# A hybrid encoder layer on one core: one more fused pair, another order of pairs, and a fifth head under way

## The chip, the cores and the metric

The kernel runs on one core of one Trainium2 chip. The metric is the device time of one execution in microseconds (us), lower is better. TensorE (PE) multiplies matrices, VectorE (DVE) and ScalarE (ACT) work elementwise, GpSimd (POOL) and SyncE (SP) issue transfers here.

## The reference, cut to what matters

```
xn = rms_norm(x, norm_g)                      # x: 256 x 4096
h = xn @ w_in                                 # w_in: 4096 x 14336
c_val, c_glu, c_gate, q, k, v, a_gate = split(h)   # seven parts of 2048 columns
conv_out = conformer_conv(c_val, c_glu, ...) * silu(c_gate)   # GLU, depthwise conv31, LayerNorm, swish
q, k = rms_norm per head (16 heads of 128)
attn = longnet_mixture(q, k, v, rel_bias)     # three dilated windows, merged by their softmax denominators
mixed = concatenate([conv_out, attn * silu(a_gate)])
y = x + mixed @ w_out                         # w_out: 4096 x 4096
```

Everything is float32. The two large products with w_in and w_out are nearly all of the work; every weight is read once.

## The kernel before, in words

**Numbers in two parts.** TensorE gets each float32 number as a high part and a low part, and a product is three products: high by high, low by high (activations' low part), high by low. The activations' parts are made once; those of the weights are made as they arrive, and this is what VectorE and ScalarE do most of the time.

**Groups, pairs and slots.** The weights are cut into 18 groups of 1024 columns: groups 0 to 3 are the convolution's values with their GLU halves, 4 and 5 its gates, 6, 7, 9 and 11 queries and keys (qk0 to qk3), 8, 10, 12 and 13 attention gates with values (agv0 to agv3), 14 to 17 the output. A group has 16 pairs; a pair is two tiles of 128 rows by 1024 columns, loaded as one tile `raw` by the SP queue, three pairs ahead. The pairs of a group are taken in the order `ORDERS[g]`, so slot 13 of a group holds pair `ORDERS[g][13]`. `raw109` is slot 13 of group 6 (16 x 6 + 13).

**A plain pair** (`plain`, L1325 and L1327) takes 24 matmuls of 128 x 512. First come 16 with the high part of the weights, `wh`, then 8 with the low part, `wl`. Its split is two casts on ScalarE (`wh`, L1131) and one subtraction on VectorE (`wl`, L1137).

**A fused pair** (`fused`) multiplies the two by two blocks of a pair by Strassen's scheme in Winograd's form: 7 products of blocks in place of 8, so 21 matmuls. Three products first (L1192 to L1194), then `m5`, `m7`, `m6` and `c21` with the high parts of `t1`, `t3`, `t2`, `t4` (two matmuls each, L1296 and L1298), then the four with the low parts (one each). Its split has four steps (`split_fused`): `b`, `b22` and three sums of blocks in place of `raw` (L1163, L1175, L1176), `t13`, `t42`; each of `b`, `b22`, `t13`, `t42` is a cast on ScalarE and a subtraction on VectorE. The sums of the activations' blocks (`xs`, `ms`) are made once for each fused pair (`block_sums`). The fused pairs of a group are listed in `FUSED[g]`: in groups 3 to 8 pairs 2, 4, 6, 8, 10, 12, 13, in group 14 pairs 0 to 3, in 15 to 17 pairs 0 to 6.

**Where the parts lie.** The parts of the weights take turns in four buffers `ws` and four more of the pool `c4`. A step of a split is put into the program as soon as a buffer is free in the order of the program (`Stream.step`, `Stream.before`), and on the chip it waits for the last matmul that reads what lay there.

**The end of a group.** The fused pairs gather the products that several blocks share in four banks of PSUM of their own, `m1`, `m5`, `m6`, `m7`. After the last fused pair `add_more` puts a copy of `m1` (ScalarE, L1359) and four additions (VectorE, L1366, L1367, L1371, L1372) into the program, one step at a time during the next plain pair (`self.add()` in `plain`), or all at once ahead of the last slot:

```
                while self.add():
                    pass
                for e in range(2):
                    for s in range(2):
                        self.before()
                        self.plain_last(u, j, rows, s, e, one)
```

In the last slot `plain_last` (L1341, L1343) finishes the four quarters of the result one after the other, 6 matmuls each, the fifth and sixth of which read `wl`. Each quarter is then taken out of PSUM (`evacuate_sum`: L981 on VectorE, L984 or L987 on ScalarE; `add_out`, L943, in the output). The next group's quarters lie in the banks that held `m1`, `m6`, `m7`, `m5`.

**Work beside the stream.** Lanes of generators (`pump`) put the rest between the matmuls: the convolution's products (`cp`, L562, `cT`, L596 and L628, `a`, L507), squares for the norms (L757), and the heads. `head_lane` has up to four heads under way at a time; each loads its bias (`T`, L789), multiplies queries and keys (`psc`, L802), takes a softmax, is turned through DRAM, and multiplies with the values (`po`, L847), then by the gate (L852). In group 14 the first fused pair waits, as the program is built, for the last head and gate (`busy()`).

Of the kernel before, what the change touches and what calls it, by code (L numbers as in the profile page):

```python
# [11 lines left out]
F32 = mybir.dt.float32  # L12
F32R = mybir.dt.float32r
# [4 lines left out]
P = 128  # L18
# [24 lines left out]
SETTLED = 3000  # L43

CP_MIN = 900
C4 = 16

X_LOAD = {0: 12, 1: 16, 3: 20, 5: 24, 6: 28}
X_SQUARE = {4: 4, 5: 0, 6: 8, 7: 12, 8: 16, 9: 20, 10: 24, 11: 28}
# [17 lines left out]
FUSED_IN = range(1, 9)  # L67
SUMS = (2, 4, 6, 8, 10, 12, 13)
FUSED = [SUMS if g in FUSED_IN else () for g in range(N_IN)]
FUSED[1], FUSED[2] = (6, 8, 12), SUMS[1:]  # L70
FUSED += [range(4)] + 3 * [range(7)]
ORDERS = N_IN * [range(16)]
ORDERS += [(8, 9, 10, 11, 12, 13, 14, 0, 15, 1, 4, 2, 5, 3, 6, 7)]
ORDERS += 3 * [(8, 9, 0, 10, 1, 11, 2, 12, 3, 13, 4, 14, 5, 6, 15, 7)]

W_SLOTS, W_MORE = 4, 4
# [61 lines left out]
def layer_kernel(  # L138
# [18 lines left out]
    sb = ctx.enter_context(tc.tile_pool(name="sb", bufs=1))  # L157
    ps = ctx.enter_context(tc.tile_pool(name="ps", bufs=1, space=bass.MemoryType.PSUM))

    def t4(name):  # L160
        return sb.tile([P, 4, 256], F32, tag="c4", bufs=C4, name=name)

    def t2(name):
        return sb.tile([P, 512], F32, tag="t2", bufs=5, name=name)

    def h2(name):
        return t2(name).rearrange("p (a b) -> p a b", a=2)
# [58 lines left out]
    def settled():  # L226

        end = now[0] + SETTLED
        while now[0] < end:
            yield  # L230
# [138 lines left out]
    def block_sums(j, src_of, parts, out, name, small=False):  # L369


        a11, a21, a12, a22 = (by_block(src_of[2 * j + k])[:, s] for k in range(2) for s in range(2))
        t = t2(f"{name}_{j}")
        s1, s2, s3, s4 = (
            t[:, P * i : P * i + P].rearrange("p (a i) -> p a i", a=4) for i in range(4)
        )
        nc.vector.tensor_sub(s1, a21, a22)
        nc.vector.tensor_sub(s2, s1, a11)
        yield 580
        nc.vector.tensor_sub(s3, a11, a21)  # L380
        nc.vector.tensor_add(s4, a12, s2)
        yield 580
        if small:
            both = [sb.tile([P, 512], F32R, tag="toep", bufs=4, name=f"{name}p{j}{i}") for i in "hl"]
        else:
            both = sb.tile([P, 2, 512], F32R, tag="c4", bufs=C4, name=f"{name}p{j}")
            both = both[:, 0], both[:, 1]
        nc.scalar.copy(both[0], t)
        yield 0, 620
        nc.vector.tensor_sub(both[1], t, both[0].bitcast(F32))  # L390
        names = {f"s{i + 1}": [b[:, P * i : P * i + P] for b in both] for i in range(4)}
        names["a11"] = [m[2 * j][:, :P] for m in parts]
        names["a12"] = [m[2 * j + 1][:, :P] for m in parts]
        names["a22"] = [m[2 * j + 1][:, P:] for m in parts]
        out[j] = names
        yield 690

    def by_block(ap):

        if len(ap.shape) == 3:  # L400
            return ap.rearrange("p t (s a i) -> p (t s) a i", s=2, a=4)
        return ap.rearrange("p (s a i) -> p s a i", s=2, a=4) if len(ap.shape) == 2 else ap
# [380 lines left out]
    def head_gen(hg, hh):  # L783
        h = 4 * hg + hh
        hs = slice(DH * hh, DH * hh + DH)
        while hg not in qk_ready:
            yield
        T = sb.tile([P, 512], F32, tag="toep", bufs=4, name=f"T{h}")
        nc.sync.dma_start(  # L789
            T[:, :384],  # L790
            bass.AP(
# [9 lines left out]
        for it in range(2):  # L801
# [7 lines left out]
        window = bass.AP(  # L809
            tensor=T.tensor, offset=T.offset + S - 1, ap=[T.ap[0], [P, 2], [-1, 256]]  # L810
        )
# [22 lines left out]
        yield from settled()  # L834
        tmp = T
        nc.vector.transpose(
# [51 lines left out]
            elif j in FUSED[-1]:  # L888
                later.append(j)

    post_lane, head_lane, gate_lane, mix_lane = Lane(2, (0,)), Lane(4), Lane(1, ()), Lane(1)
    fetch_lane, ag_lane = Lane(1, (1,)), Lane(1, ())
    conv_lane, ln_lane, cp_lane = Lane(1, ()), Lane(1, (0,)), Lane(1, (1,))
    center_lane = Lane(1, (1,))
# [103 lines left out]
    def post(g, e, tile_, pair):  # L998
        kind, idx = groups[g][:2]
        if kind == "conv" and e == 1:  # L1000
            post_lane.add(glu_post(idx, tile_))
        elif kind == "gate":
            post_lane.add(gate_post(2 * idx + e, tile_))
        elif kind == "agv" and e == 0:
            ag_lane.add(ag_post(idx, tile_))
        elif kind == "agv":
            vt[idx] = pair
        elif kind == "qk" and e == 0:
            qt[idx] = tile_
        elif kind == "qk":  # L1010
            kt[idx] = tile_
            post_lane.add(qk_norm(idx))
            for hh in range(4):
                head_lane.add(head_gen(idx, hh))
# [30 lines left out]
    class Stream:  # L1045
# [24 lines left out]
        def tile(self, name, of, tag):  # L1070

            self.held[tag] += 1
            self.tags.setdefault(of, []).append(tag)
            bufs, n = (W_SLOTS, 2048) if tag == "ws" else (C4, 1024)
            return sb.tile([P, n], F32R, tag=tag, bufs=bufs, name=name)
# [378 lines left out]
def _layout(i):  # L1454


    def cols(a):
        return a.reshape(-1, P).T

# [4 lines left out]
    for g, (kind, _, *firsts) in enumerate(GROUPS):  # L1464
# [4 lines left out]
        for j in FUSED[g]:  # L1469
            jj = (j + n_pairs // 2) % n_pairs if kind == "out" else j  # L1470
            b = w[g, jj].reshape(P, 4, 512)
            w[g, jj] = b[:, (0, 2, 3, 1)].reshape(P, 2, 2, 512)
    x_cols = i["x"][0].T.reshape(KT, P, S).transpose(1, 0, 2).reshape(P, KT * S)
    vecs = [i[n][0] for n in ("conv_b", "conv_ln_g", "conv_ln_b", "q_norm_g", "k_norm_g")]
# [4 lines left out]
        "vecs": np.concatenate([cols(v) for v in vecs], axis=1),  # L1479
        "conv_w": i["conv_w"][0].T.reshape(16, P, TAPS).transpose(1, 0, 2).reshape(P, -1),  # L1480
        "bias_rows": np.concatenate(
# [32 lines left out]
```

## Time and profile before

| what | us |
|---|---|
| median of three runs | 1561.62 |
| the three runs | 1560.17, 1561.62, 1565.84 |
| the profiled execution | 1561.59 |
| its span on the core | 1559.8 |
| TensorE busy | 1554.2 |
| VectorE busy | 1350.8 |
| ScalarE busy | 1017.3 |
| GpSimd busy | 148.5 |

The span is what the trace covers; 1.8 us of the profiled execution lie around it. Busy time of an engine is the time in which it runs instructions, so TensorE has 5.6 us without a matmul in the span. The granted clock is 1.00 of 2.4 GHz from end to end.

### The profile page before, as it was taken

Reading aid. Unit: us, or ns where it says so; the run is one execution under the profiler, and the core shown is the slowest. Engines: PE = TensorE matmul, PEld = TensorE weight load, DVE = VectorE, ACT = ScalarE, POOL = GpSimd, SP = SyncE. Lnnn points to the kernel's source line nnn. Section 1 sums busy time; section 2 is a strip of 40 time slices with the busy share of each in tenths; the row PEclk is TensorE's granted clock in tenths of the full one; section 3 lists DMA queues with packets and bytes.
Section 4 is the critical chain, followed back from the end, with each engine's and each line's share of the span. In section 5 each row is a group of like instructions: output and inputs, shape, how many; then the busy total and the mean of one; then the engine's idle time right before and its main releaser. Section 6 shows DMA issues by size and latency. Waiting matters only on the chain.

```text
span 1559.8 us, 18654 instructions
## 1 busy us (share of the span) xinstructions
PE 1554.2 (100%) x6844; PEld 1285.2 (82%) x6844; DVE 1350.8 (87%) x1449; ACT 1017.3 (65%) x1564; POOL 148.5 (10%) x222
## 2 busy tenths in 40 slices
PE   9999999999999999999999999999999999999998
PEld 8888888888888888888888888888888888888887
DVE  7898799989899888999897989886676798998988
ACT  7665556767676677677778887776657654555453
POOL 0000000101010100001120012010240200000000
PEclk9999999999999999999999999999999999999999
DMA  9556567969788887789695668665886866666663
GB/s 350 199 201 231 189 218 241 274 218 267 241 258 254 243 246 256 228 247 251 226 313 188 230 229 266 213 230 203 251 270 209 252 223 230 239 217 240 234 240 119
DMA packets 80828, 367.91 MB, mean 236 GB/s; under 512 B 9152, under 2 KB 31296, under 8 KB 44128
## 3 DMA queue, kind: packets, MB, share of 16 engines
q1 hardware_dynamic: 50336, 317.86, 57.9%
q0 software_dynamic: 30112, 48.58, 14.3%
q8 instruction: 53, 0.87, 0.2%
q14 instruction: 39, 0.32, 0.1%
q10 hardware_dynamic: 288, 0.28, 0.1%
HBM read 328.57 MB, written 18.91 MB: 223 GB/s over the span
## 4 chain that ended last, share of the span: by engine, by line
PE 94%; DVE 2%; DMA 1%; issue 1%; ACT 1%; DVEq 0%; SPq 0%; ACTq 0%
PE c L1325 40%; PE c L1327 20%; PE m L1296 6%; PE c L1341 4%; PE m L1298 3%; PE c L1296 2%; PE c L1193 2%; PE c L1194 2%; PE c L1192 2%; PE c L1343 2%; PE acc L1033 2%; PE acc L1034 2%; PE acc L1036 2%; DMA raw<-in_w_dram 1%; PE c L1298 1%
## 5 line engine op out<-in xcount | busy, mean ns | idle before, releaser
L1137 DVE TENSOR_TENSOR wl<-raw,wh 128x2048 fp32r<-128x2048 f32 x196 | 448.2, 2289 | 146.9 <-ACT wh L1131 140.3
L1131 ACT CAST wh<-raw 128x1024 fp32r<-128x1024 f32 x392 | 390.7, 1047 | 194.0 <-PE c L1327 124.0
L1325 PE MATMUL c<-wh,nh 128*128 128x512 f32 x1152 | 450.2, 391 | 0.0
L1327 PE MATMUL c<-wh,nl 128*128 128x512 f32 x1152 | 448.4, 389 | 0.0
L1154 ACT CAST t<-raw 128x1024 fp32r<-128x1024 f32 x152 | 160.1, 1053 | 250.3 <-DVE raw L1163 171.1
L1325 PE MATMUL c<-wl,nh 128*128 128x512 f32 x1152 | 287.7, 392 | 0.0
L1325 PEld LDWEIGHTS c<-wh,nh 128*128 128x128 f32 x1152 | 216.3, 188 | 45.2
L1327 PEld LDWEIGHTS c<-wh,nl 128*128 128x128 f32 x1152 | 216.3, 188 | 45.1
L1325 PEld LDWEIGHTS c<-wl,nh 128*128 128x128 f32 x1152 | 216.3, 188 | 44.9
L1155 DVE TENSOR_TENSOR t<-raw,t 128x1024 fp32r<-128x1024 f32 x152 | 185.5, 1222 | 3.7 <-ACT t L1154 0.4
L562 ACT ACTIVATE cp<-a,wT 128x241 f32<-128x241 f32 (+14 forms) x312 | 131.4, 491 | 1.0 <-DVE cT L619 1.0
L1325 PE MATMUL c<-wh,mh 128*128 128x512 f32 x280 | 109.1, 390 | 0.0
L1327 PE MATMUL c<-wh,ml 128*128 128x512 f32 x280 | 108.9, 389 | 0.0
L581 POOL DMA_DIRECT2D cT<-cp x38 | 48.8, 1285 | 533.7 <-ACT cp L562 488.7
L1163 DVE TENSOR_TENSOR raw<-raw 128x1024 f32<-128x1024 f32 x76 | 93.1, 1225 | 2.6
L1155 DVE TENSOR_TENSOR b<-raw,b 128x1024 fp32r<-128x1024 f32 x76 | 92.7, 1220 | 1.6 <-ACT b L1154 1.0
L1154 ACT CAST b<-raw 128x1024 fp32r<-128x1024 f32 x76 | 79.6, 1047 | 3.5 <-PE c L1327 1.8
L1296 PE MATMUL m<-t,xsp 128*128 128x512 f32 x216 | 72.3, 389 | 0.0
L628 DVE SCALAR_TENSOR_TENSOR cT<-a,wT,cT 128x255 f32<-128x255 f32 (+8 forms) x168 | 68.9, 476 | 0.6
L1325 PE MATMUL c<-wl,mh 128*128 128x512 f32 x280 | 69.2, 389 | 0.0
L1327 PEld LDWEIGHTS c<-wh,ml 128*128 128x128 f32 x280 | 52.6, 188 | 10.9
L1325 PEld LDWEIGHTS c<-wl,mh 128*128 128x128 f32 x280 | 52.6, 188 | 10.9
(346 smaller groups left out, 2311.0 us busy)
## 6 DMA issues: line engine op xcount, KB each, us to landing
raw<-in_w_dram SPq DMA_DIRECT2D x286, 1024.0 KB, 5.0
xr<-in_x_dram SPq DMA_DIRECT2D x8, 512.0 KB, 6.5
out_dram<-xr SPq DMA_DIRECT2D x15, 256.0 KB, 7.5
xT<-in_x_cols_dram SPq DMA_DIRECT2D x7, 512.0 KB, 9.0
T<-bias_dram SPq DMA_DIRECT2D x16, 192.0 KB, 6.1
cT<-cp POOLq DMA_DIRECT2D x4, 488.0 KB, 6.7
cT<-cp POOLq DMA_DIRECT2D x4, 486.0 KB, 6.7
cT<-cp POOLq DMA_DIRECT2D x4, 484.0 KB, 6.1
```

The source lines that it names most:

```text
L562: nc.scalar.activation(cp[:, t, lo:hi], a[:, t, lo + sh : hi + sh], AF.Copy, scale=wT[:, 4 * cb + t, k : k + 1],)
L628: nc.vector.scalar_tensor_tensor(c[:, t, lo:hi], a[:, t, lo + sh : hi + sh], wT[:, 4 * cb + t, k : k + 1], c[:, t, lo:hi], op0=ALU.mult, o ...
L1131: nc.scalar.copy(h, raw_tiles[u][:, k])
L1137: nc.vector.tensor_sub(l, src, h.bitcast(F32))
L1154: nc.scalar.copy(h, src)
L1155: nc.vector.tensor_sub(l, src, h.bitcast(F32))
L1163: nc.vector.tensor_add(r[:, 0:4:3, :], r[:, 0:3:2, :], twice(r[:, 3, :]))
L1296: nc.tensor.matmul(acc, ah, b, start=begin, stop=end)
L1298: nc.tensor.matmul(acc, al, b, start=False, stop=False)
L1325: nc.tensor.matmul(acc, a[s][0], b[e], start=begin, stop=False)
L1327: nc.tensor.matmul(acc, a[s][1], b[e], start=False, stop=False)
L1341: nc.tensor.matmul(acc, a[s][0], b[e], start=False, stop=end)
```

## The change

Five things, all in tables and pool sizes:

- In groups 3 to 8 (`FUSED_IN[2:]`) pairs 13 and 14 change places: slot 13 holds the plain pair 14, and slot 14 the fused pair 13. Before, the fused pairs 12 and 13 stood in slots 12 and 13 and the plain pairs in 14 and 15.
- In group 14 pair 4 is fused too, and the order is new: the fused pairs stand in slots 6, 8, 10, 12, 14 in place of 7, 9, 11, 13.
- Up to five heads are under way in place of four.
- `T` and the small sums (`toep`) get five buffers in place of four, and the tiles of 128 x 512 (`t2`) six in place of five.
- The pool `c4` has 15 buffers in place of 16.

```diff
-C4 = 16
+C4 = 15
...
-FUSED += [range(4)] + 3 * [range(7)]
+FUSED += [range(5)] + 3 * [range(7)]
 ORDERS = N_IN * [range(16)]
-ORDERS += [(8, 9, 10, 11, 12, 13, 14, 0, 15, 1, 4, 2, 5, 3, 6, 7)]
+for _g in FUSED_IN[2:]:
+    ORDERS[_g] = (*range(13), 14, 13, 15)
+ORDERS += [(8, 9, 10, 11, 12, 13, 0, 14, 1, 15, 2, 5, 3, 6, 4, 7)]
...
-        return sb.tile([P, 512], F32, tag="t2", bufs=5, name=name)
+        return sb.tile([P, 512], F32, tag="t2", bufs=6, name=name)
...
-            both = [sb.tile([P, 512], F32R, tag="toep", bufs=4, name=f"{name}p{j}{i}") for i in "hl"]
+            both = [sb.tile([P, 512], F32R, tag="toep", bufs=5, name=f"{name}p{j}{i}") for i in "hl"]
...
-        T = sb.tile([P, 512], F32, tag="toep", bufs=4, name=f"T{h}")
+        T = sb.tile([P, 512], F32, tag="toep", bufs=5, name=f"T{h}")
...
-    post_lane, head_lane, gate_lane, mix_lane = Lane(2, (0,)), Lane(4), Lane(1, ()), Lane(1)
+    post_lane, head_lane, gate_lane, mix_lane = Lane(2, (0,)), Lane(5), Lane(1, ()), Lane(1)
```

The changed file has two lines more ahead of the functions, so that L1359 of before is L1361 of the changed kernel.

ScalarE before, at the end of group 6: the last fused pair is `109` (slot 13), `110` and `111` are plain, `112` is the first pair of group 7, and the copy of `m1` is the first step of `add_more`.

```order
L1154 CAST t42_1090_4456<-raw109_4332 128x1024
L1131 CAST wh110_4475<-raw110_4368 128x1024 x2
L1131 CAST wh111_4490<-raw111_4411 128x1024 x2
L1359 COPY qk0_0_4521<-m1_6_4047 128x512
L1131 CAST wh112_4537<-raw112_4460 128x1024 x2
L757 ACTIVATE sq0_0_0_4581,ssqk0_4580<-qk0_0_4521 128x128
```

The same place on ScalarE in the changed kernel, where `110` is the last fused pair:

```order
L1156 CAST t42_110_4479<-raw110_4368 128x1024
L1133 CAST wh111_4501<-raw111_4411 128x1024 x2
L1133 CAST wh112_4535<-raw112_4443 128x1024 x2
L1361 COPY qk0_0_4541<-m1_6_4046 128x512
L759 ACTIVATE sq0_0_0_4581,ssqk0_4580<-qk0_0_4541 128x128
L759 ACTIVATE sq0_0_1_4583,ssqk0_4580<-qk0_0_4541 128x128
```

The copy of `m1` stood ahead of the next group's first cast (`wh112`) and now stands behind it. It is so in groups 3 to 8 and, for the copy of group 14, ahead of group 15.

VectorE before, at the same end of group 6, from the last step of the fused pair `109` on:

```order
L1155 TENSOR_TENSOR t13_109_4447<-raw109_4332,t13_109_4447 128x1024
L1155 TENSOR_TENSOR t42_1091_4457<-raw109_4332,t42_1090_4456 128x1024
L1137 TENSOR_TENSOR wl110_4480<-raw110_4368,wh110_4475 128x2048
L1137 TENSOR_TENSOR wl111_4506<-raw111_4411,wh111_4490 128x2048
L1366 TENSOR_TENSOR us6_4520<-qk0_0_4521,m6_6_4049 128x512
L1367 TENSOR_TENSOR qk0_0_4521<-us6_4520,m7_6_4050 128x512
L1371 TENSOR_TENSOR qk0_1_4522<-m5_6_4048,us6_4520 128x512
L1372 TENSOR_TENSOR qk0_1_4522<-m5_6_4048,qk0_0_4521 128x512
L1137 TENSOR_TENSOR wl112_4548<-raw112_4460,wh112_4537 128x2048
L981 TENSOR_TENSOR qk0_0_4521<-qk0_0_4521,c11_6_3960 128x512
```

VectorE in the changed kernel:

```order
L1157 TENSOR_TENSOR t13_110_4474<-raw110_4368,t13_110_4474 128x1024
L1157 TENSOR_TENSOR t42_110_4479<-raw110_4368,t42_110_4479 128x1024
L1139 TENSOR_TENSOR wl111_4512<-raw111_4411,wh111_4501 128x2048
L1368 TENSOR_TENSOR us6_4540<-qk0_0_4541,m6_6_4048 128x512
L1369 TENSOR_TENSOR qk0_0_4541<-us6_4540,m7_6_4049 128x512
L1373 TENSOR_TENSOR qk0_1_4542<-m5_6_4047,us6_4540 128x512
L1374 TENSOR_TENSOR qk0_1_4542<-m5_6_4047,qk0_0_4541 128x512
L1139 TENSOR_TENSOR wl112_4548<-raw112_4443,wh112_4535 128x2048
L983 TENSOR_TENSOR qk0_0_4541<-qk0_0_4541,c11_6_3958 128x512
```

One `wl` fewer stands between the last fused pair's split and the last slot's `wl111`, and between it and the additions that need the fused pair's banks; the additions still stand ahead of the next group's first `wl112`.

TensorE before, in group 14 ahead of its first fused pair (slot 7, `m1_14`), from the low part of slot 6 on; `po15` is the last head, and `po12` to `po14` stand some 65 rows further ahead:

```order
L1325 MATMUL c12_14_9568<-wl230_9829,mh14_9562 128x512
L1325 MATMUL c22_14_9569<-wl230_9829,mh14_9562 128x512
L1325 MATMUL c12_14_9568<-wl230_9829,mh14_9562 128x512
L1325 MATMUL c22_14_9569<-wl230_9829,mh14_9562 128x512
L847 MATMUL po15_9905<-pr15_9377,agv3_1_9551 128x256 x2
L1192 MATMUL m1_14_9917<-b_2310_9833,mh0_8948 128x512
```

TensorE in the changed kernel, in group 14 ahead of its first fused pair, now slot 6:

```order
L849 MATMUL po13_9841<-pr13_9231,agv3_1_9579 128x256 x2
L849 MATMUL po14_9844<-pr14_9244,agv3_1_9579 128x256 x2
L849 MATMUL po15_9847<-pr15_9293,agv3_1_9579 128x256 x2
L1327 MATMUL c11_14_9595<-wl229_9776,mh13_9508 128x512
L1327 MATMUL c21_14_9596<-wl229_9776,mh13_9508 128x512
L1327 MATMUL c11_14_9595<-wl229_9776,mh13_9508 128x512
L1327 MATMUL c21_14_9596<-wl229_9776,mh13_9508 128x512
L1327 MATMUL c12_14_9597<-wl229_9776,mh13_9508 128x512
L1327 MATMUL c22_14_9598<-wl229_9776,mh13_9508 128x512
L1327 MATMUL c12_14_9597<-wl229_9776,mh13_9508 128x512
L1327 MATMUL c22_14_9598<-wl229_9776,mh13_9508 128x512
L1194 MATMUL m1_14_9881<-b_2300_9780,mh0_8960 128x512
```

All four last heads stand together now, 8 matmuls ahead of the first fused pair, which begins one plain pair earlier.

## Rows read from the trace of the kernel before

**Rows 1.** The page: busy time, share of the span, instructions of each engine.

```profile
PE 1554.2 (100%) x6844; PEld 1285.2 (82%) x6844; DVE 1350.8 (87%) x1449; ACT 1017.3 (65%) x1564; POOL 148.5 (10%) x222
```

**Rows 2.** What TensorE waited for in the whole span.

```profile
PE spin L1399 <- DVE ones L174: 1.1, 1, 1.1
PE m L1296 <- ACT t L1154: 0.5, 1, 0.5
```

**Rows 3.** Timeline of TensorE, group 6, slots 11 to 13: start, duration, instruction.

```profile
571.46 1.98 PE L1325 MATMUL c<-wl,nh 128*128 128x512 f32 x8
573.27 0.39 PE L1192 MATMUL m<-b,nh 128*128 128x512 f32 x1
...
580.93 0.40 PE L1298 MATMUL m<-t,xsp13l 128*128 128x512 f32 x1
581.80 0.50 PE L1296 MATMUL m<-t,xsp13h 128*128 128x512 f32 x1 [0.48 <-ACT t L1154]
```

**Rows 4.** Timeline of VectorE, group 6, slots 11 to 13.

```profile
567.05 2.29 DVE L1137 TENSOR_TENSOR wl<-raw,wh 128x2048 fp32r<-128x2048 f32 x1 [2.64 <-ACT wh L1131]
...
573.10 0.69 DVE L1176 TENSOR_TENSOR raw<-raw 128x512 f32<-128x512 f32 x1
...
579.98 0.69 DVE L1176 TENSOR_TENSOR raw<-raw 128x512 f32<-128x512 f32 x1
```

**Rows 5.** Timeline of ScalarE, group 6, slots 10 to 13.

```profile
563.05 2.08 ACT L596 ACTIVATE cT<-a,vec_cols,wT 128x256 f32<-128x256 f32 x4
...
580.70 1.05 ACT L1154 CAST t<-raw 128x1024 fp32r<-128x1024 f32 x1 [0.95 <-DVE raw L1176]
```

**Rows 6.** Timeline of TensorE, groups 4 and 5: last slot, low parts of slots 1 and 11.

```profile
423.41 0.39 PE L1341 MATMUL c<-wh,nh 128*128 128x512 f32 x1
...
437.92 0.84 PE L1325 MATMUL c<-wl,nh 128*128 128x512 f32 x3
...
488.92 1.07 PE L1325 MATMUL c<-wl,nh 128*128 128x512 f32 x4
```

**Rows 7.** Timeline of VectorE from group 4 to group 5, and slot 11 of group 5.

```profile
419.94 0.68 DVE L1366 TENSOR_TENSOR us<-gate,m 128x512 f32<-128x512 f32 x1
...
421.86 0.68 DVE L1372 TENSOR_TENSOR gate<-m,gate 128x512 f32<-128x512 f32 x1
423.83 2.29 DVE L1137 TENSOR_TENSOR wl<-raw,wh 128x2048 fp32r<-128x2048 f32 x1 [1.29 <-ACT wh L1131]
426.04 1.28 DVE L981 TENSOR_TENSOR gate<-gate,c 128x512 f32<-128x512 f32 x2
...
432.33 2.29 DVE L1137 TENSOR_TENSOR wl<-raw,wh 128x2048 fp32r<-128x2048 f32 x1 [1.37 <-ACT wh L1131]
...
481.90 2.29 DVE L1137 TENSOR_TENSOR wl<-raw,wh 128x2048 fp32r<-128x2048 f32 x1 [0.68 <-ACT wh L1131]
```

**Rows 8.** Timeline of ScalarE from group 4 to group 5.

```profile
418.55 0.57 ACT L1359 COPY gate<-m 128x512 f32<-128x512 f32 x1
...
429.77 0.63 ACT L984 ACTIVATE gate<-gate 128x512 f32<-128x512 f32 x1 [0.73 <-DVE gate L981]
430.31 1.98 ACT L1131 CAST wh<-raw 128x1024 fp32r<-128x1024 f32 x2
```

**Rows 9.** Timeline of VectorE, slot 1 of groups 4 and 7.

```profile
348.13 2.29 DVE L1137 TENSOR_TENSOR wl<-raw,wh 128x2048 fp32r<-128x2048 f32 x1
...
597.16 2.29 DVE L1137 TENSOR_TENSOR wl<-raw,wh 128x2048 fp32r<-128x2048 f32 x1 [1.58 <-ACT wh L1131]
```

**Rows 10.** Timeline of TensorE, low part of slot 1 of groups 4 and 7.

```profile
355.38 0.84 PE L1325 MATMUL c<-wl,nh 128*128 128x512 f32 x3
...
603.75 0.62 PE L1325 MATMUL c<-wl,nh 128*128 128x512 f32 x2
```

**Rows 11.** Timeline of VectorE, group 14: the first fused pair's last step.

```profile
1260.33 2.35 DVE L1155 TENSOR_TENSOR t<-raw,t 128x1024 fp32r<-128x1024 f32 x2
```

**Rows 12.** Timeline of TensorE, group 14: start of the first fused pair.

```profile
1262.37 0.58 PE L1192 MATMUL m<-b,mh 128*128 128x512 f32 x1
```

## The prediction

> **What bounds the kernel now.** I read the page first: TensorE is busy for 1554.2 of 1559.8 us [rows 1], so only its own work, or a wait that it does not have yet, can change the time. Then its waits: 1.1 us at the start and one of 0.5 us [rows 2]. All the rest is matmuls at an even pace: eight of them, 571.46 to 573.27, make 0.2266 us each [rows 3], so a plain pair of 24 takes 5.44 us and a fused one of 21 takes 4.76. VectorE is busy for 87% [rows 1], and what it and ScalarE do for a pair has to be ready ahead of TensorE. The reader should therefore look in the timelines for one thing: how far ahead. I call **lead** the time from the end of a plain pair's `wl` on VectorE to the first matmul that reads it. In slot 11 of group 5 it is 488.92 - (481.90 + 2.29) = 4.73 us [rows 6, 7], in slot 11 of group 6 it is 571.46 - 569.34 = 2.12 us [rows 3, 4].
>
> **What lead is needed.** Behind `wl` VectorE does `b` and the sums of `raw`, which end at 573.79 [rows 4], 4.45 after the `wl`; then ScalarE casts `t42`, 1.05 us [rows 5]. TensorE reads that cast 21 matmuls, 4.76 us, after the first low matmul of the slot ahead (8 low ones, then 13 of the fused pair). 4.45 + 1.05 + some 0.1 for two handovers - 4.76 gives 0.85 us: with less lead than this in a slot that a fused pair follows, TensorE waits for the difference. The one stall shows that this counting works. Between neighbouring fused pairs VectorE needs 579.98 - 573.10 = 6.88 us [rows 4] where TensorE takes 4.76, so 2.12 is lost; 2.12 - 0.85 - 2.12 = -0.85 is forecast for slot 13 of group 6, and the row shows 581.80 - 580.93 - 0.23 = 0.64 lost [rows 3]. Two slots of plain and fused take TensorE 10.20 us; the chain from one `wl` to the next takes 4.45 + 1.05 + 1.98 (the two casts `wh`) + 2.29 + 0.1, 9.87. So a lead lost comes back by some 0.35 us every two slots; group 5 goes from 3.30 in slot 1 to 4.73 in slot 11 that way, with one step without gain.
>
> **What the change gives.** A fifth fused pair in group 14 takes out 3 matmuls: 3 x 0.2266 = 0.68 us. No two fused pairs are neighbours in group 6: 0.64. The other groups' neighbours cost nothing now, since [rows 2] has one such wait. For the 0.68 I take the row. The Trainium skill, "TensorE: Matmul & The Clock Gate", section "Back-to-back issue gap", gives about 131 ns for a matmul of 512 columns in a sustained stream; the three would give 0.39 by it, and the time would be 0.3 us longer. The trace disagrees at 227 ns, and I stay with it.
>
> **What it moves at the ends of groups.** Let T be the start of the last slot's matmuls, 423.41 in group 4 [rows 6]. Now the copy of `m1` is at T - 4.9 [rows 8], the additions from T - 3.5 to T - 0.9, the next group's first `wl` ends at T + 2.7, and the `wl` of its slot 1 at 434.62, T + 11.2; it is needed at 437.92, T + 14.5 [rows 6, 7]: lead 3.30. In the changed order the copy stands behind two casts of the next group. Their buffer is that of `t13` of the last fused pair, which the third last matmul ahead of T reads, so they start at T - 0.2. Two casts 1.98, copy 0.57 [rows 8]: T + 2.35. Additions, 421.86 + 0.68 - 419.94 = 2.60 [rows 7]: T + 4.95. `wl`, 2.2 to its successor's start: T + 7.15. Four evacuations, two of which take 1.28 [rows 7]: T + 9.6. Then ScalarE's pass over the last quarter 0.63, the casts of slot 1 1.98 [rows 8], and the `wl` 2.29: about T + 14.45. The lead is 0.05, so TensorE loses 0.85 - 0.05 = **0.8 us at 4 to 5, and the same at 5 to 6**, which has the same operations. No PSUM bank is late: the first bank given back by the additions is needed at T + 5.9, the last at T + 7.7, and they end at T + 4.95.
>
> Elsewhere the same shift, some 3.3 to 3.8 us, meets more lead. Slot 1 of group 4 has 355.38 - 350.42 = 4.96 [rows 9, 10], and keeps 1.2. Slot 1 of group 7 has 603.75 - 599.45 = 4.30 [rows 9, 10] and keeps some 0.5, and more if group 6 ends late (below). Group 8 is like 4, within 0.1 us of the limit; group 9 has no fused pairs, and VectorE needs 2.29 there for 5.44 of TensorE. From 14 to 15 the eight operations of `add_more` end near T + 6, the first `wl` at T + 8.2 against T + 9.07. For all of these I take **0.1 us**.
>
> **What it moves inside.** The last slot now follows a fused pair, and its quarters read `wl` after 4 matmuls, not after 16: 12 x 0.2266 = 2.72 us of lead go. With the gain of 0.35, slot 15 needs 2.37 in slot 13. Group 3 is entered as before; group 4 starts from 1.2 and grows by 6 steps to over 3. Group 5 starts from 0.85 and gains 5 steps: 2.6, just enough. Group 6 starts from 0.85 too, but the convolution's `cT` stands between two links of its chain, 2.08 us [rows 5]; in slot 11 it has 2.12 where group 5 has 4.73, 2.61 less. So 0.85 + 4 x 0.35 - 2.61 = -0.36 there: TensorE loses 0.85 + 0.36 = **1.2 us** at slots 11 and 12. Slot 13 then has 1.2, slot 15 has 1.2 + 0.35 - 2.72 = -1.15: **1.15 us** more at the last slot, which group 7 finds as lead. Groups 7 and 8, with their squares and norms spread over ScalarE's gaps, keep some 2.4 or more in slot 13.
>
> **The fused pairs of group 14.** The first fused split ends at 1262.68 [rows 11], 0.3 us after `m1` starts [rows 12], and the low part of `t42` is read 19 matmuls, 4.3 us, after `m1`: 4 us in hand. One slot earlier is 5.44 us earlier, and as the lists of the section on the change show, a `wl` is gone ahead of it; the sums for pair 6 and the gating of the last heads go behind it too, some 7 us in all. I take nothing. The fifth head starts work early and saves at most the changeover between heads and stream; nothing. Its cost could be a head's load landing late; from nothing to the 0.9 us of a stall like those above, I take nothing: in the order of TensorE the closest head's turned operand is asked for 31 matmuls, 7.0 us, ahead of its use, against 33 before. One buffer of `c4` fewer against two small ones more: nothing, as the buffers handed to the weights stay at four.
>
> **Sum.** 0.8 + 0.8 + 0.1 + 1.2 + 1.15 = 4.05 lost, 0.68 + 0.64 = 1.32 gained: +2.7 us on the execution's own 1561.59 (span 1559.8 and 1.8 around it), which is the median of the runs, 1561.62, within 0.03. That gives 1564.3. Each of the four stalls rests on differences good to 0.2 us, as the -0.85 against 0.64 shows, and a stall in one place is lead in the next.
>
> **Rivals.**
> *Only the gains.* The shift is absorbed, because the needed lead is smaller than 0.85, or the copy is not held so long. For it: the formula was 0.2 too strict in group 6, and the shifts are of the size of the leads. Against it: the casts stand ahead of the copy in the list. 1561.6 - 1.3 = 1560.3. The Trainium skill, "TensorE: Matmul & The Clock Gate", section "Architectural detail: the array is 16× 32×32, not 1× 128×128", says that ScalarE and VectorE take their queues strictly in order and that only TensorE can pull weight loads ahead; by that the copy cannot pass the casts, and this rival needs the leads instead. Chance 0.25.
> *Leads don't come back.* If the chain of 9.87 us takes 10.2 once the convolution's casts `cp` stand in it, every group from 4 to 8 meets its last slot with 0.85 - 2.72: 1.9 us each, 5 x 1.9 = 9.5, with the 1.7 at the boundaries 11.2 less 1.3: 1571.5. It decides once the gain per two slots falls under 0.1 us. Against it: group 5's leads grew with these casts in it. Chance 0.06.
> *The change does not do what it says in group 14.* The fifth pair is fused in the program, but the heads or their sums come late, and TensorE waits at the first fused pair for the four last heads to be gated; each VectorE operation behind them (1.5 us for four, 2.3 with a `wl`) is paid. 1564.3 + 3 = 1567.3. Against it: the 4 us in hand. Chance 0.07.
> The forecast itself has 0.62.
>
> **The numbers.** Half a per cent, 7.8 us, is about what a measurement of this kernel can tell from no change; the three runs already differ by 5.7. Forecast, only-gains and group 14 all lie inside: same 0.92. Slower holds the second rival and a little of a group 14 that goes worse: 0.07. Faster by 7.8 us isn't to be had where TensorE has 5.6 us without work: 0.01. The range goes from the only-gains case, with 0.3 for the order of the sum's errors, to 1568.5, where the third rival and one more boundary of 0.8 end; it leaves out the second.
>
> **What would show it.** 3 matmuls fewer; no wait in the pairs 12 and 13 for a neighbour; waits of TensorE for `wh` or `t` in slots 1 and 2 of groups 5 and 6, for `wh` and `t` at slots 11 and 12 of group 6, and for `wl` (L1343) at its last slot, together near 4 us; the copy of `m1` 2 us after T in groups 3 to 8; no wait ahead of `m1` in group 14. Wrong would be: no waits at all (the first rival), waits for `wl` at every last slot (the second), or a wait at `m1` of group 14 (the third).

## The result, and the profile after

The changed kernel takes 1564.68 us, median of 20 runs (1563.36 to 1566.78), the kernel before 1560.51, median of 20 (1560.10 to 1565.84). The ratio is 1.0024, with a 95% interval of 1.0018 to 1.0031: a quarter of a per cent slower, 4.2 us by the medians. The ratios leave out one run, of e10 below, which took 2874.52 us at a granted clock of 0.77. The forecast was 1564.3. The profiled execution took 1564.29 us, with a span of 1562.5.

The page and TensorE's waits of the changed kernel, which answer to [rows 1] and [rows 2]:

```profile
PE 1555.6 (100%) x6841; PEld 1282.8 (82%) x6841; DVE 1353.3 (87%) x1457; ACT 1016.5 (65%) x1563; POOL 149.7 (10%) x223
```

```profile
PE spin L1401 <- DVE ones L176: 1.1, 1, 1.1
PE c L1343 <- DVE wl L1139: 0.6, 1, 0.6
PE c L1327 <- DVE wl L1139: 0.5, 1, 0.5
PE acc L1035 <- ACT wh L1108: 0.2, 1, 0.2
PE c L1327 <- ACT wh L1133: 0.2, 1, 0.2
```

Three matmuls fewer, and where one wait stood there are several. Most of them are too short for this view. They show when one takes, for each group, the time from its first matmul to the next group's first. That is the ruler of this study: it repeats to 0.04 us from kernel to kernel wherever nothing was changed, with two exceptions. Group 6 takes 82.67 to 83.29 with its order unchanged, and with five heads groups 10 to 13 differ from execution to execution (e9 below). Each kernel has one profiled execution, so in these places a figure is good for that execution only. In us, each against the profiled execution of before:

| group | before | changed | what it holds |
|---|---|---|---|
| 4 | 82.54 | +0.08 | |
| 5 | 82.54 | +0.91 | waits in slots 1 and 2 |
| 6 | 83.29 | +1.48 | waits in slots 1, 2, 12, 15; the neighbours' wait of before gone |
| 8 | 82.54 | +0.17 | |
| 9 | 90.51 | +0.77 | a wait in slot 1, and short ones |
| 10 to 13 | 370.71 | +0.59 | a wait for `wl` in group 11; heads moved from 12 to 11 |
| 14 | 87.86 | -0.72 | 3 matmuls fewer, no wait |
| 2, 3, 7, 15 to 17 | | +0.04 together | |

The sum is +3.3. The span grew by 2.7, since the start up to group 2 was 0.60 shorter in this execution.

**From group 4 to 5.** The timeline of ScalarE in the changed kernel, which answers to [rows 8]:

```profile
422.61 2.00 ACT L1133 CAST wh<-raw 128x1024 fp32r<-128x1024 f32 x2 [0.73 <-PE m L1298]
424.52 0.58 ACT L1361 COPY gate<-m 128x512 f32<-128x512 f32 x1
430.57 2.43 ACT L986 ACTIVATE gate<-gate 128x512 f32<-128x512 f32 x4 [5.47 <-DVE gate L983]
432.90 1.97 ACT L1133 CAST wh<-raw 128x1024 fp32r<-128x1024 f32 x2
```

The timeline of VectorE there, which answers to [rows 7]:

```profile
420.40 2.29 DVE L1139 TENSOR_TENSOR wl<-raw,wh 128x2048 fp32r<-128x2048 f32 x1 [0.67 <-ACT wh L1133]
425.12 0.69 DVE L1368 TENSOR_TENSOR us<-gate,m 128x512 f32<-128x512 f32 x1 [2.43 <-ACT gate L1361]
...
427.65 2.28 DVE L1139 TENSOR_TENSOR wl<-raw,wh 128x2048 fp32r<-128x2048 f32 x1
429.85 2.48 DVE L983 TENSOR_TENSOR gate<-gate,c 128x512 f32<-128x512 f32 x4
...
434.91 2.29 DVE L1139 TENSOR_TENSOR wl<-raw,wh 128x2048 fp32r<-128x2048 f32 x1 [1.96 <-ACT wh L1133]
```

And TensorE's, which answers to [rows 6]:

```profile
422.88 0.40 PE L1343 MATMUL c<-wh,nh 128*128 128x512 f32 x1
...
433.98 0.50 PE L1327 MATMUL c<-wh,nh 128*128 128x512 f32 x1
434.32 0.40 PE L1329 MATMUL c<-wh,nl 128*128 128x512 f32 x1
...
437.78 1.98 PE L1327 MATMUL c<-wl,nh 128*128 128x512 f32 x8
...
442.31 0.39 PE L1300 MATMUL m<-t,xsp 128*128 128x512 f32 x1
442.84 0.50 PE L1298 MATMUL m<-t,xsp 128*128 128x512 f32 x1
443.17 0.39 PE L1300 MATMUL m<-t,xsp 128*128 128x512 f32 x1
```

T, the start of the last slot's matmuls, is 422.88. VectorE is free at 422.69, waits 2.43 us for the copy behind two casts, and starts the additions at T + 2.24 (forecast 2.35). The `wl` of slot 1 ends at T + 14.32 (forecast 14.45). TensorE then loses 0.19 at the first matmul of slot 1 and 0.30 at `t42` in slot 2, and 0.11 at the matmul behind each, 0.71 in all; the rest of group 5's 0.91 is matmuls at a pace slower by up to 0.03 us each. The lead in slot 1, 437.78 - 437.20, is 0.58, and what TensorE still loses at `t42` says how much was needed: 0.88.

**The end of group 6.** VectorE and TensorE of the changed kernel:

```profile
589.56 2.29 DVE L1139 TENSOR_TENSOR wl<-raw,wh 128x2048 fp32r<-128x2048 f32 x1 [0.67 <-ACT wh L1133]
592.42 0.69 DVE L1368 TENSOR_TENSOR us<-qk,m 128x512 f32<-128x512 f32 x1 [0.57 <-ACT qk L1361]
```

```profile
590.86 0.40 PE L1345 MATMUL c<-wh,nl 128*128 128x512 f32 x1
591.90 0.73 PE L1343 MATMUL c<-wl,nh 128*128 128x512 f32 x2 [0.64 <-DVE wl L1139]
592.47 0.39 PE L1343 MATMUL c<-wh,nh 128*128 128x512 f32 x1
```

The last slot's fifth matmul waits for a `wl` that ends at 591.85: 0.81 us, and 0.11 behind it.

**In group 11**, which the forecast did not have, VectorE and TensorE of the changed kernel:

```profile
955.18 1.30 DVE L489 STREAM_TRANSPOSE turn_qk<-qk 128x512 f32<-128x512 f32 x2 [5.80 <-DMA turn_ag1d<-turn_ag]
...
957.47 2.28 DVE L1139 TENSOR_TENSOR wl<-raw,wh 128x2048 fp32r<-128x2048 f32 x1
```

```profile
958.93 0.39 PE L1329 MATMUL c<-wh,nl 128*128 128x512 f32 x1
959.81 1.20 PE L1327 MATMUL c<-wl,nh 128*128 128x512 f32 x4 [0.49 <-DVE wl L1139]
```

A turn into a `c4` tile stands until the transfer that reads another `c4` tile is done, and a `wl` stands behind it.

### The profile page after: what moved, and what is told of

The parts are those of the page before. It is cut to its first block, busy times and chain, and to the rows that moved or that the text cites. A ratio compares the mean times of both kernels' runs of the same rounds, so it can differ in the third digit from the quotient of the medians.

```text
span 1562.5 us, 18652 instructions
## 1 busy us (share of the span) xinstructions
PE 1555.6 (100%) x6841; PEld 1282.8 (82%) x6841; DVE 1353.3 (87%) x1457; ACT 1016.5 (65%) x1563; POOL 149.7 (10%) x223
## 4 chain that ended last, share of the span: by engine, by line
PE 87%; issue 5%; DVE 3%; ACT 3%; DMA 2%; SPq 0%; POOL 0%; DVEq 0%; ACTq 0%; POOLq 0%
PE c L1327 36%; PE c L1329 18%; PE m L1298 6%; PE c L1343 3%; PE m L1300 3%; PE c L1195 2%; PE c L1298 2%; PE c L1196 2%; PE c L1194 2%; PE acc L1035 2%; PE acc L1036 2%; PE acc L1038 2%; ACT wh L1133 2%; PE c L1345 1%; PE c L1300 1%
## 5 line engine op out<-in xcount | busy, mean ns | idle before, releaser
L564 ACT ACTIVATE cp<-a,wT 128x244 f32<-128x244 f32 (+14 forms) x308 | 129.7, 491 | 14.0 <-DVE cT L621 13.8
L1327 PE MATMUL c<-wh,mh 128*128 128x512 f32 x272 | 105.8, 389 | 0.0
L1327 PEld LDWEIGHTS c<-wh,mh 128*128 128x128 f32 x272 | 51.0, 188 | 10.6
```

Source lines behind the costliest of these rows:

```text
L564: nc.scalar.activation(cp[:, t, lo:hi], a[:, t, lo + sh : hi + sh], AF.Copy, scale=wT[:, 4 * cb + t, k : k + 1],)
L1327: nc.tensor.matmul(acc, a[s][0], b[e], start=begin, stop=False)
```

## The experiments

Theory, from here on: the time goes where leads run out, at the ends of groups 4 to 8, since the copy of `m1` stands behind a cast and the last slot behind a fused pair. First rival: the fifth head and the pools cost it. Second rival, for the waits themselves: only one of the two, copy or last slot, matters. All medians are of 4 to 12 runs of the kernel; the kernel before, run beside them, had medians of 1560.7 to 1561.2. The ratio comes from all runs and differs from the quotient of the medians by up to 0.0011.

| run | median us | ratio to before, 95% | 4 to 8 | 9 | 10 to 13 | 14 |
|---|---|---|---|---|---|---|
| changed | 1564.68 | 1.0024 (1.0018 to 1.0031) | +2.66 | +0.77 | +0.59 | -0.72 |
| e1_orders | 1564.39 | 1.0016 (1.0008 to 1.0025) | +2.72 | +0.21 | -0.18 | +0.04 |
| e2_heads | 1564.42 | 1.0014 (1.0006 to 1.0023) | -0.62 | 0 | +2.43 | -0.04 |
| e3_out | 1561.35 | 1.0000 (0.9991 to 1.0008) | -0.24 | 0 | 0 | +0.53 |
| e4_c4 | 1573.20 | 1.0067 (1.0049 to 1.0086) | -0.21 | 0 | +12.13 | 0 |
| e5_copy | 1560.27 | 0.9996 (0.9987 to 1.0005) | -0.64 | 0 | +0.37 | -0.72 |
| e6_low | 1564.52 | 1.0022 (1.0013 to 1.0031) | +2.06 | +0.47 | +1.15 | -0.72 |
| e7_pools | 1575.60 | 1.0094 (1.0080 to 1.0109) | +2.60 | +0.24 | +12.81 | -0.72 |
| e8_out | 1561.32 | 1.0007 (0.9998 to 1.0016) | -0.13 | 0 | 0 | +0.53 |
| e9_noorder | 1563.67 | 1.0017 (1.0008 to 1.0025) | -0.50 | 0 | +4.36 | -0.72 |
| e10_copy_orders | 1561.20 | 0.9997 (0.9988 to 1.0006) | +0.25 | 0 | -0.18 | +0.04 |
| e11_c4_14 | 1573.61 | 1.0084 (1.0070 to 1.0098) | +5.47 | +0.18 | +7.79 | -0.72 |
| e12_both | 1561.93 | 1.0006 (0.9997 to 1.0015) | -0.65 | 0 | +1.69 | -0.72 |

The last four columns are group durations of the profiled execution less those of the profiled execution of before, in us.

**e1_orders: the order of groups 3 to 8 alone.**

```diff
 ORDERS = N_IN * [range(16)]
+for _g in FUSED_IN[2:]:
+    ORDERS[_g] = (*range(13), 14, 13, 15)
```

> Only the new order of pairs in groups 3 to 8; group 14, the heads and the pools as before. Group-end theory (the copy of m1 behind the next group's cast costs 3.7 us of lead at each boundary, and the last slot 2.7 more): the loss is all here, group by group as in the changed kernel's trace: group 5 +0.9, 6 +1.5 net, 8 +0.2, 9 +0.8, together +3.4 us on before, 1563.9. Rival (the fifth head and the pools cost the time, the order only takes away group 6's stall): -0.7, 1559.8.

Groups 4 to 8 are what they are in the changed kernel (group 5 +0.87, 6 +1.60, 8 +0.21). The first rival's 1559.8 is out. Group 9 has +0.21 here. It has +0.47, +0.24 and +0.18 in e6, e7 and e11, which have the fifth head like the changed kernel, so what made that kernel's +0.77 stays open.

**e2_heads: the fifth head and the pools alone** (lines shortened).

```diff
-C4 = 16
+C4 = 15
...
-tag="t2", bufs=5
+tag="t2", bufs=6
...
-tag="toep", bufs=4
+tag="toep", bufs=5
...
-head_lane = Lane(4)
+head_lane = Lane(5)
```

> Only the fifth head and the pool sizes (toep 5, t2 6, c4 15); orders and fused pairs as before. Group-end theory: at most the one wait for wl that the changed kernel shows in group 11, 0.6 us: 1560.5 to 1561.1. Rival (the heads cost the time): +3.4 or more, 1564.

The rival's time came: the median is 1564.42, and the profiled execution, at 1562.54, was the fastest of the twelve. The heads do cost, 2.4 us in groups 10 to 13 of that execution, and alone they cost as much as the order alone, which takes 1564.39. TensorE's waits of this kernel show `po` behind a transfer.

```profile
PE po L847 <- DMA pr<-turn_p3d: 1.6, 1, 1.6
...
PE po L847 <- DMA pr<-turn_p4d: 0.6, 1, 0.6
```

In front of it VectorE stands in the same place as in the changed kernel:

```profile
DVE turn_qk L487 <- DMA turn_ag1d<-turn_ag: 5.5, 1, 5.5
```

**e3_out: group 14 alone.**

```diff
-FUSED += [range(4)] + 3 * [range(7)]
+FUSED += [range(5)] + 3 * [range(7)]
...
-ORDERS += [(8, 9, 10, 11, 12, 13, 14, 0, 15, 1, 4, 2, 5, 3, 6, 7)]
+ORDERS += [(8, 9, 10, 11, 12, 13, 0, 14, 1, 15, 2, 5, 3, 6, 4, 7)]
```

> Only group 14: five fused pairs and its new order; four heads, pools as before. Group-end theory: 3 matmuls fewer and no wait, -0.7 us, 1559.8, group 14 shorter by 0.7. Rival (the first fused pair waits for the last heads when it comes one slot earlier): a wait ahead of m1 in group 14, 1560.5 or more.

The rival is nearer. With four heads the last four heads stand not 8 matmuls ahead of the first fused pair but directly in front, and the bank of the last one is `m6`'s. TensorE and VectorE of this kernel in group 14:

```profile
1252.88 3.61 PE L847 MATMUL po<-pr,agv 128*128 128x256 f32 x16
1256.15 0.58 PE L1192 MATMUL m<-b,mh 128*128 128x512 f32 x1
...
1259.10 0.39 PE L1298 MATMUL m<-t,msp 128*128 128x512 f32 x1
1260.50 0.47 PE L1296 MATMUL m<-t,msp 128*128 128x512 f32 x1 [1.01 <-DVE agv L852]
```

```profile
1255.59 1.07 DVE L852 TENSOR_TENSOR agv<-agv,po 128x256 f32<-128x256 f32 x3
...
1259.94 0.41 DVE L852 TENSOR_TENSOR agv<-agv,po 128x256 f32<-128x256 f32 x1
```

Three of the four gatings run at once, the fourth stands behind the sums of another pair, and TensorE loses 1.2 us for the 0.7 it gains. So in this order the fused pair pays only together with the fifth head, which brings all four gatings to the front: in the changed kernel, in e5, e6, e7, e9, e11 and e12, all with five heads, group 14 is 0.72 shorter, in e3 it is 0.53 longer.

**e4_c4: one c4 buffer fewer, nothing else.**

```diff
-C4 = 16
+C4 = 15
```

> Only the pool c4 at 15 buffers in place of 16; every engine's order stays word for word that of before. If the missing buffer makes the wait for wl in group 11 (a turn into a c4 buffer that a transfer still reads): such a wait here too, about 0.6 us, 1561.1. If that wait comes from the fifth head: no wait, 1560.5.

Neither. With the order of before, the missing buffer costs 12 us, in groups 12 and 13; one of the six runs took 1566.41, the others 1573.04 to 1575.87. Waits of TensorE, then of VectorE, of this kernel (VectorE's in the whole span, only some):

```profile
PE po L847 <- DMA pr<-turn_p10d: 5.2, 1, 5.2
PE c L1325 <- DVE wl L1137: 2.8, 1, 2.8
```

```profile
DVE turn_qk L487 <- PE psc L802: 9.2, 1, 9.2
...
DVE turn_qk L487 <- DMA turn_ag1d<-turn_ag: 2.9, 1, 2.9
```

Before has neither `turn_qk` wait. A turn of queries and keys needs a `c4` tile, and with 15 it waits until the last head's product or a transfer gives one back; what stands behind it on VectorE waits too.

**e5_copy: the changed kernel, the copy ahead of the next group's cast.**

```diff
+            self.limit = NG * n_pairs
...
+            if not self.todo or self.todo[0][2] > self.limit:
+                return False
...
+                    if last and slot == 14:
+                        self.limit = u + 1
                     self.fused(u, sums[j], one, more, first, last)
...
                 while self.add():
                     pass
+                self.limit = NG * n_pairs
```

> The changed kernel, but the split of the next group may enter the program only once the last fused pair's additions are in it, so that the copy of m1 stands ahead of the next group's cast on ScalarE. Group-end theory (the copy behind the cast costs the lead): the lead in slot 1 of groups 5 and 6 goes from 0.6 to over 2 us, the losses of groups 5, 6, 8 and 9 (0.9, 2, 0.2, 0.8) go, and with the longer lead group 6's last slot too; -3.4 us on the changed kernel, 1561.3. Rival (the last slot behind a fused pair is what costs): the waits in slots 1 and 2 go, but TensorE still waits 0.9 for wl in group 6's last slot, 1562.2 or more.

As the theory said, in each group: 5 +0.02, 6 -0.73, 8 +0.02, 9 0.00. Up to group 13 the orders of TensorE, VectorE and GpSimd are those of the changed kernel, and ScalarE's differs only where the copy moved. The boundary from 4 to 5, ScalarE and VectorE of this kernel:

```profile
420.25 0.57 ACT L1367 COPY gate<-m 128x512 f32<-128x512 f32 x1
423.00 2.01 ACT L1136 CAST wh<-raw 128x1024 fp32r<-128x1024 f32 x2 [2.19 <-PE m L1304]
```

```profile
423.30 0.69 DVE L1374 TENSOR_TENSOR us<-gate,m 128x512 f32<-128x512 f32 x1 [2.15 <-PE m L1304]
...
433.09 2.29 DVE L1142 TENSOR_TENSOR wl<-raw,wh 128x2048 fp32r<-128x2048 f32 x1 [1.97 <-ACT wh L1136]
```

The additions no longer wait for the copy but for the last product of the fused pair, and slot 1 has a lead of 2.43 us in place of 0.58. Group 6's last slot, too, is free of its wait, with 0.15 of lead to spare, so the second rival is out as far as it takes the last slot alone. This is the fastest kernel of the study in the median; its interval holds 1.

**e6_low: the changed kernel, the last slot's low parts later.** The two quarters of each half get their high parts first, then both their low parts.

```diff
-        def plain_last(self, u, j, rows, s, e, one):
-            acc = one[f"c{s + 1}{e + 1}"]
+        def plain_last(self, u, j, rows, e, one):
             for part in "hl":
                 for k, (a, b) in enumerate(self.blocks_of(u, j, rows, part)):
                     end = part == "l" and k == 1
+                    for s in range(2):
+                        acc = one[f"c{s + 1}{e + 1}"]
...
```

> The changed kernel, but the last slot multiplies the high parts of two quarters before the low parts of both, so that wl is read after 8 matmuls and not after 4 (0.9 us later). If the wait in group 6's last slot is the 2.7 us of lead that the slot lacks behind a fused pair: it goes, -0.8, 1563.9, and the other groups stay. Rival (that wait only passes on what the boundaries lost): it turns up in slot 1 or 2 of group 7, and the time stays at 1564.7.

Group 6 is 0.60 shorter than in the changed kernel, no wait for `wl` at a last slot is left, and groups 5, 7 and 8 stay within 0.04: the wait was the last slot's own. The time stays at 1564.52 all the same. In the profiled execution groups 10 to 13 are 0.56 longer, group 9 is 0.30 shorter, and the end of the kernel is 0.7 longer, which is the edit's own price: two quarters of the last group are now done at once, and more is left for VectorE behind the last matmul. Its last rows in the changed kernel, then in this one:

```profile
1558.61 0.75 DVE L945 TENSOR_TENSOR xr<-xr,c 128x256 f32<-128x256 f32 x2 [0.67 <-PE c L1343]
```

```profile
1557.90 1.35 DVE L945 TENSOR_TENSOR xr<-xr,c 128x512 f32<-128x512 f32 x3 [1.44 <-PE c L1345]
```

**e7_pools: the changed kernel with the pools of before**, so c4 16, toep 4, t2 5.

> The changed kernel with the pools of before (c4 16, toep 4, t2 5); the orders of PE, VectorE and ScalarE stay word for word the same. If the missing c4 buffer makes the wait for wl in group 11: groups 11 and 12 together 0.6 us shorter, 1564.1. If it is the fifth head: no change there, or longer, since the fifth head's bias now waits for a toep buffer.

Groups 11 and 12 together are +0.05, against +0.62 in the changed kernel: the wait for `wl` in group 11 and VectorE's wait for `turn_ag1d` are gone, with every engine's order unchanged. So the missing `c4` buffer made it, and e11, with one fewer still, has more of it. The fifth head pays elsewhere without the other two pools' buffers: 9.0 us in group 10 and 3.7 in group 13. The DMA queue of SP, and a wait of VectorE in group 13 of this kernel:

```profile
SPq L791 <- DMA turn_p0d<-T: 18.3, 1, 18.3
```

```profile
DVE pr L814 <- PE po L849: 12.2, 1, 12.2
```

In group 10 a head's `T` load waits 18.3 us for its `toep` buffer at the head of the queue that also loads the weights, and the weights stand behind it: TensorE then waits 5.9 us for a `wh`. In group 13 VectorE waits 12.2 us to write a head's `pr`, which is a `t2` tile, until the product `po` that reads an earlier `pr` is done, and TensorE waits 3.2 us for a `wl` behind it. So by this wait the second price is the missing `t2` buffer's, and not the `toep` buffer's; no run takes either alone.

**e8_out: five fused pairs in the kernel before's group 14**, the first at slot 7, two of them neighbours.

```diff
-ORDERS += [(8, 9, 10, 11, 12, 13, 14, 0, 15, 1, 4, 2, 5, 3, 6, 7)]
+ORDERS += [(8, 9, 10, 11, 12, 13, 14, 0, 15, 1, 5, 2, 3, 6, 4, 7)]
```

> The kernel before with five fused pairs in group 14, the first one at slot 7 as before, the others at 9, 11, 12, 14 (two neighbours). Theory of leads: group 14 has 4.5 us of lead or more there and neighbours need 3.0, so no wait; 3 matmuls fewer, -0.7 us, 1560.3. Rival (neighbours cost their 2.1 us, or the fifth sum comes late): a wait in slots 9 to 13 of group 14, 1561 or more.

The rival's time, but not its place, and by my own rule: I had left out the 2.7 us that a last slot behind a fused pair lacks. After neighbours and then a fused pair in slot 14 TensorE waits 0.7 us for `wl` at the last slot. The neighbours themselves cost only some 0.1 at one matmul.

**e9_noorder: the changed kernel without the order of groups 3 to 8.**

```diff
-for _g in FUSED_IN[2:]:
-    ORDERS[_g] = (*range(13), 14, 13, 15)
```

> The changed kernel without the new order in groups 3 to 8 (five heads, its pools and group 14 as changed). Group-end theory: groups 4 to 9 as before, so 3.3 us less than the changed kernel, 1561.4; group 14 keeps its -0.7, groups 11 and 12 their +0.6 (up to +2.4, as the heads alone gave). Rival (the heads' part grows once the order's waits are gone, since waits hand out lead): 1563 or more.

Groups 4 to 9 are as before, as the theory said, but the heads take 4.4 us in groups 10 to 13 of this execution, and the median is the rival's, 1563.67, of runs that lie between 1561.13 and 1566.41. The wait of VectorE for `turn_ag1d` is here too (6.2 us). Behind it TensorE stands 0.6 us at a `wl` and 2.0 us at a `po`, and then runs at half its clock for over three us (engine columns PE, PEld, DVE, ACT, POOL, then the granted clock, 0.50):

```profile
964.10:967.40 3.30, 3.30 (x10) 2.56 (x9) 3.30 (x3) 2.75 (x5) 2.62 (x5) 0.50 0.96 338
```

e2 has the same orders of all engines up to group 13 and lost only 2.43 there, with a granted clock of 1.00. So what the heads cost in one execution is no measure of a kernel to within 2 us, and the rival's reason, that waits hand out lead, is not shown. The parts don't add: by the medians the order alone takes 3.4, the heads and pools alone 3.4, and all together 4.2. The new order does spare the heads something, since e5, with the same heads and pools and no wait at the ends of groups, stayed under 1561.8 in ten of eleven runs; how it does so is not shown.

**e10_copy_orders: the kernel before with the new order and the copy ahead.** The edits of e1 and e5 together.

> The kernel before with the new order in groups 3 to 8 and the copy of m1 ahead of the next group's cast; four heads, pools and group 14 as before. Group-end theory: no waits in groups 3 to 9, group 6 as in the kernel with all parts (-0.7 on the profiled execution of before), so 1560.3 to 1561.0: the order itself is worth nothing or the one small wait. Rival (a last slot behind a fused pair costs by itself): waits for wl at last slots, 1562.

Groups 5 and 8 are free of waits. Group 6 has one of 0.6 at its last slot, which had 0.15 of lead in e5, so the last slot does cost, by itself and where the convolution's `cT` comes in. Time and interval are those of the kernel before: the order gains nothing that can be measured.

**e11_c4_14: the changed kernel with one c4 buffer fewer still.**

> The changed kernel with c4 at 14 buffers in place of 15, the orders of all engines word for word the same. If c4 is what holds the turns through DRAM in groups 10 to 13: more and longer waits there, groups 10 to 13 longer by 3 us or more, 1568 or more. If 15 is already past the point where c4 matters: 1564.7.

As the first sentence said, and it starts earlier than named there: +2.75 in group 8 already, +7.79 in groups 10 to 13. In group 11 VectorE now waits twice in a row for a turn:

```profile
957.13 1.31 DVE L489 STREAM_TRANSPOSE turn_qk<-qk 128x512 f32<-128x512 f32 x2 [6.83 <-DMA turn_ag1d<-turn_ag]
961.72 1.31 DVE L489 STREAM_TRANSPOSE turn_qk<-qk 128x512 f32<-128x512 f32 x2 [3.28 <-DMA turn_qk2d<-turn_qk]
```

**e12_both: e5 and e6 together.**

> The changed kernel with both mends: the copy of m1 ahead of the next group's cast, and the last slot's low parts read after 8 matmuls. Group-end theory: groups 3 to 9 without a wait, and 0.9 us more lead at each last slot than with the copy alone, so group 6 can't fall short there (-0.7); group 14 -0.7, groups 11 and 12 +0.4: 1560.0 to 1560.5, half a us under the kernel before. Rival (the later low parts hold back the evacuations and with them the next group): slot 1 of a group waits again, 1561 or more.

Groups 3 to 9 are as forecast, group 6 at -0.73. But groups 10 to 13 take +1.69 in place of e5's +0.37, with waits for `wl` (0.9) and at a `po` (0.4), the end of the kernel is 0.7 longer as in e6, and 1561.93 is not better than e5. The rival's place is wrong, its time right, and its reason holds at the very end, where evacuations come late.

## Why the prediction was right, and where it was not

**What bounds it, and leads as the measure: right.** The waits for `t` and `wl` in groups 4 to 8 stand where a lead fell under what was needed, and the needed 0.85 was measured as 0.88; the 0.19 at the first matmul of slot 1 is the same shift in ScalarE's `wh`, which the lead does not count. None of the prediction's rivals came: there were waits, there was none at `m1` of group 14, and lead came back, in group 5 from 0.58 in slot 1 to 3.05 in slot 13.

**Boundaries 4 to 5 and 5 to 6: right.** 0.8 each was forecast; 0.71 and 0.67 were lost in the waits (5 to 6: two waits of 0.19 and 0.26 and 0.11 behind each). e5 shows the cause, since moving the copy alone takes all of it away. The Trainium skill, "TensorE: Matmul & The Clock Gate", section "Architectural detail: the array is 16× 32×32, not 1× 128×128", has ScalarE and VectorE take their queues strictly in order. The trace agrees: VectorE stood 2.43 us at the first addition, and the next `wl`, whose casts had ended at 424.61, came behind the additions at 427.65.

**Slot 12 of group 6: too large.** 1.2 was forecast, 0.39 lost (0.27 and 0.12 behind it). The step "2.61 less than group 5" took the lead in slot 11 of two different groups as the price of `cT`. In the changed kernel the lead falls from 2.15 in slot 9 to 0.58 in slot 11, so `cT` costs 1.6 and with the usual gain some 1.9; the rest of the 2.61 was already gone in slot 9 of before, 3.72 against 4.36 in group 5, and what took it is not shown.

**The last slot of group 6: right in place, 0.92 for 1.15.** e6 takes 0.6 of it away by reading `wl` 0.9 us later; e10 has it without any wait at the boundaries.

**The gain from neighbours: right in this execution, not in most.** Group 6 of the kernel before took 83.29 in the profiled execution, but 82.67 to 83.16 in four others that leave its order as it is (e2, e3, e4, e8) and 82.79 in e9. So the stall of [rows 3] was partly that execution's. It accounts for 0.1 to 0.6 of the 1.1 us by which 1561.59 stood above the later median of 1560.51, and the start up to group 2 was longer there than in all other profiled executions but e1's, by 0.15 to 0.82.

**Elsewhere at the boundaries: 8 to 9 was missed.** 0.1 was forecast for all. Group 9 lost 0.77, 0.45 of it at the first matmul of slot 1, which waited for a cast of `wh`, and at the one behind it: I had looked at VectorE alone in a group without fused pairs, and ScalarE, with a table load of 1.28 us ahead of the casts and the copy, was late. With the copy ahead of the cast (e5) all of it is gone; why it is 0.18 to 0.47 in e1, e6, e7 and e11, which have the copy behind the cast too, is open.

**Pools: wrong.** "One buffer of `c4` fewer: nothing" was argued from the buffers handed to the weights. The turns through DRAM take theirs from the same pool, and 0.57 us went by that in groups 11 and 12 (+0.62, against +0.05 in e7). With the order of before and four heads it was 12 us (e4).

**Group 14: right, for a reason I had not seen.** -0.72 for the -0.68 forecast. I had counted the fifth head as worth nothing there; e3 shows that without it the fused pair loses more than it gives.

**The sum.** Forecast losses of 4.05 and gains of 1.32; in the trace, groups 4 to 8 lost 2.66 net for a forecast of 3.4, and groups 9 to 13 lost 1.4 for a forecast of nearly nothing. Two errors of about a us met, and the forecast was nearer than its steps: +2.7 forecast, +2.7 between the two profiled executions. By the medians the change is +4.2, not +2.7, and the forecast of 1564.3 came so near to 1564.68 because the 1561.59 that it started from, backed by three runs, was 1.1 us too high. That part is luck. How much the heads cost in groups 10 to 13 with five heads and 15 `c4` buffers (0.37 to 4.36 us in one execution each) is not settled.

## What to carry to other kernels

Where one engine is busy all the time, measure how far ahead the others are at each step, and book every edit against that lead: what it shifts, what a place needs, and how fast a lead comes back. When work moves to the last place before a boundary, look at what the next stage has already queued ahead of the work that follows it: here an early cast ahead of the copy cost 3.3 us over groups 4 to 8 (+2.66 against -0.64 in e5), and holding it back cost nothing. Pools that several stages share are part of the schedule; taking one buffer that the stage at hand does not need can stall another stage by more than the edit gives.

## What was not expected of the hardware

After some waits TensorE ran at half its clock for a while. In e11 it stood 5.1 us in group 11; the busy time by stretches (engine columns PE, PEld, DVE, ACT, POOL in us, then the granted clock) and the timeline of TensorE:

```profile
950.00:961.00 11.00, 11.00 (x50) 9.20 (x49) 1.61 (x3) 2.27 (x6) 1.66 (x3) 1.00 0.62 213
...
967.00:970.00 3.00, 3.00 (x9) 2.35 (x8) 2.96 (x6) 2.98 (x5) 2.75 (x6) 0.50 0.97 266
970.00:980.00 10.00, 10.00 (x41) 8.16 (x40) 8.66 (x11) 4.82 (x10) 3.66 (x7) 0.89 1.02 249
```

```profile
966.34 3.78 PE L1327 MATMUL c<-wl,nh 128*128 128x512 f32 x8 [4.91 <-DVE wl L1139]
969.92 0.63 PE L1327 MATMUL c<-wh,nh 128*128 128x512 f32 x1
```

The granted clock is 1.00 (2.4 GHz) before the wait, 0.50 (1.2 GHz) after it and 0.89 over the ten us that follow; eight matmuls take 3.58 us to the next start, where they took 1.81 [rows 3]. So this wait cost some 1.8 us more than its own length in those eight alone. The granted clock was 0.50 too behind the waits of 2.8 and 5.2 us in e4 and of 5.9 in group 10 of e7, so part of what these kernels lose is clock. Here the length of one wait did not tell: it was 0.50 in e9 behind 0.6 and 2.0 us, and 1.00 behind the 3.2 us in group 13 of e7. The short waits of the changed kernel, 0.2 to 0.8 us, cost 0.11 at the next matmul and little behind it, at a granted clock of 1.00.
